# Rotating images by 90 degrees: two of the twelve slabs loaded in rows of 8 KB instead of 16 KB

## The chip, the cores and the metric

The kernel runs on one core of one Trainium2 chip. The metric is the device time in microseconds (us) of one execution. Ratios are computed as the mean time of one kernel's fast runs over that of the kernel before in the same rounds on the same chip, so they are not quite the ratio of the medians that are quoted beside them.

## The reference

The input is `x`, float32 of 32 x 3 x 256 x 256, 25.17 MB. The output has the same size, each image turned by 90 degrees:

```python
def reference(x):
    return np.rot90(x, k=-1, axes=(-2, -1)).astype(np.float32)
```

There is no arithmetic: 25.17 MB come in, 25.17 MB go out, and VectorE rearranges them in between.

## The kernel before

The 96 images are taken in 12 slabs of 8 images (2 MiB). A slab is loaded with two transfers of 1 MiB, in one of two forms. In the *plain* form a transfer fills all 128 partitions with 8 image rows (8 KB, one packet) each. In the *wide* form it fills every second partition with 16 rows (16 KB, one packet), and the second transfer fills the others. Two transposes a slab turn it; their access patterns depend on the form, and their result is the same, so that the stores are the same: 8 KB from each partition.

```python
    RI, RO = 16, 8
    ld8_v = rows_in.rearrange("(n i p r) w -> n p i (r w)", i=I, p=P, r=RO)
    ld16_v = rows_in.rearrange("(n i m r) w -> n i m (r w)", i=I, m=Q * K, r=RI)
    # ... one buffer per slab; 12 x 16 KB in each partition
    for n in range(n_slabs):
        for i in range(I):
            if n in (0, last):
                nc.sync.dma_start(out=units[n][:, i], in_=ld8_v[n][:, i])
            else:
                nc.sync.dma_start(out=units[n][i::I].rearrange("p i f -> p (i f)"), in_=ld16_v[n, i])

    for n in range(n_slabs):
        t_in, t_out = units[n], units[n - 1] if n else turned0
        if n in (0, last):
            # ... two transposes of the plain form
        else:
            # ... two transposes of the wide form
        # ... stores of slab n: slab 1 as 128 KB, 896 KB and 1 MiB, slabs 2 and 3 as 2 x 1 MiB, the rest 2 MiB
    # ... slab 0, turned in PSUM, is copied back by ScalarE and stored last
```

## Time and profile before

| what | value |
|---|---|
| time before, three runs | 123.51, 123.54, 123.78 us |
| span of the profiled execution | 122.3 us |

The prediction below shows the page and the stretches. The waits of the DMA queue (columns: who waited, for what, us in total, times, longest):

```profile
SPq L65 <- DMA u<-in_x_dram: 25.5, 13, 2.0
...
SPq L87 <- DMA u<-in_x_dram: 8.3, 4, 2.1
```

An issue waits for the landing of an earlier transfer. In the trace eight completion semaphores (counters that tell that a transfer has landed) go round among the transfers, so that transfer number j is issued when number j - 8 has landed. That gives a clock: the issue times of the stores are the landing times of the loads eight places ahead. The second view is the timeline of the kernel before around the turn from loads to stores (columns: start, duration, engine, line, operation):

```profile
44.87 0.35 SPq L82 DMA_DIRECT2D out_dram<-u  x1
47.39 0.34 SPq L83 DMA_DIRECT2D out_dram<-u  x1
49.81 0.33 SPq L84 DMA_DIRECT2D out_dram<-u  x1
52.32 7.65 SPq L87 DMA_DIRECT2D out_dram<-u  x4
59.69 1.28 ACT L92 ACT_TABLE_LOAD   x1 [59.69 <-DMA u<-in_x_dram]
62.67 3.31 SPq L89 DMA_DIRECT2D out_dram<-u  x3
```

ScalarE is released at 59.69 us by the first half of the last slab, and the issue at 62.67 us waits for its second half. So the last load of 1 MiB took 62.67 - 59.69 = 2.98 us. Between the issues before it lie 2.42 to 2.52 us.

### The profile page before, as it was taken

Reading aid. Unit: us, or ns where it says so; the run is one execution under the profiler, and the core shown is the slowest. Engines: PE = TensorE matmul, PEld = TensorE weight load, DVE = VectorE, ACT = ScalarE, POOL = GpSimd, SP = SyncE. Lnnn points to the kernel's source line nnn. Section 1 sums busy time; section 2 is a strip of 40 time slices with the busy share of each in tenths; the row PEclk is TensorE's granted clock in tenths of the full one; section 3 lists DMA queues with packets and bytes.
Section 4 is the critical chain, followed back from the end, with each engine's and each line's share of the span. In section 5 each row is a group of like instructions: output and inputs, shape, how many; then the busy total and the mean of one; then the engine's idle time right before and its main releaser. Section 6 shows DMA issues by size and latency. Waiting matters only on the chain.

```text
span 122.3 us, 138 instructions
## 1 busy us (share of the span) xinstructions
DVE 93.3 (76%) x24; ACT 5.0 (4%) x3; POOL 0.2 (0%) x4
## 2 busy tenths in 40 slices
DVE  0199999999999999999999999999999940000000
ACT  0000000000000000000400000000000641000000
POOL 0000000000000000000000000000000000000000
DMA  3999999999999999999999999999999999999994
GB/s 118 418 450 429 429 429 429 429 429 429 429 429 429 429 429 429 429 429 391 359 413 429 429 429 426 429 421 429 429 429 429 429 429 429 429 429 426 429 429 180
DMA packets 5632, 50.33 MB, mean 412 GB/s; under 512 B 640, under 2 KB 768, under 8 KB 896
## 3 DMA queue, kind: packets, MB, share of 16 engines
q1 hardware_dynamic: 5632, 50.33, 97.8%
HBM read 25.17 MB, written 25.17 MB: 412 GB/s over the span
## 4 chain that ended last, share of the span: by engine, by line
DVE 47%; issue 27%; DMA 4%; DVEq 3%; ACT 2%
DVE u L79 37%; DVE turned L73 6%; DMA u<-in_x_dram 4%; DVE u L73 3%; DVEq L119 3%; ACT u L92 2%
## 5 line engine op out<-in xcount | busy, mean ns | idle before, releaser
L79 DVE STREAM_TRANSPOSE u<-u 128x2048 f32<-128x2048 f32 x20 | 78.0, 3949 | 0.3
L73 DVE STREAM_TRANSPOSE turned<-u 128x2048 f32<-128x2048 f32 x2 | 7.6, 3828 | 5.6 <-DMA u<-in_x_dram 5.6
L73 DVE STREAM_TRANSPOSE u<-u 128x2048 f32<-128x2048 f32 x2 | 7.7, 3953 | 0.0
L92 ACT COPY u<-turned 128x2048 f32<-128x2048 f32 x2 | 3.7, 1866 | 36.5 <-DVE u L73 36.5
L92 ACT ACT_TABLE_LOAD x1 | 1.3, 1283 | 59.7 <-DMA u<-in_x_dram 59.7
L108 POOL MEMSET const-bfloat16-1.0<- 128x1 bf16 x1 | 0.1, 102 | 0.0
L108 POOL MEMSET const-uint8-127<- 128x1 uint8 x1 | 0.1, 102 | 0.0
L108 POOL MEMSET const-float32-0.0<- 128x1 f32 x1 | 0.1, 99 | 0.2 <-issue 0.2
L108 POOL MEMSET const-float32-1.0<- 128x1 f32 x1 | 0.1, 99 | 0.0
## 6 DMA issues: line engine op xcount, KB each, us to landing
u<-in_x_dram SPq DMA_DIRECT2D x24, 1024.0 KB, 19.6
out_dram<-u SPq DMA_DIRECT2D x9, 2048.0 KB, 23.0
out_dram<-u SPq DMA_DIRECT2D x5, 1024.0 KB, 17.7
out_dram<-u SPq DMA_DIRECT2D x1, 896.0 KB, 17.8
out_dram<-u SPq DMA_DIRECT2D x1, 128.0 KB, 18.3
```

The lines of the kernel that those rows point to most:

```text
L73: nc.vector.transpose(out=dst[:, :, ::-1, ::-1], in_=src)
L79: nc.vector.transpose(out=dst[:, cs], in_=src[:, cs])
L92: nc.scalar.copy(out=units[last][:, i], in_=turned0[:, i])
L108: nc = _bacc.Bacc("TRN2", target_bir_lowering=False, num_devices=1)
L119: with _tile.TileContext(nc) as tc:
```

## The change

The intent: the plain form was used for the first and the last slab, and it is now used for the last three (6 MiB) and the first, so that slabs 9 and 10 (4 MiB) change. Loads and transposes change their form together; bytes, number of transfers and order stay.

```diff
+    plain = (0, last - 2, last - 1, last)
...
-            if n in (0, last):
+            if n in plain:
                 nc.sync.dma_start(out=units[n][:, i], in_=ld8_v[n][:, i])
...
-        if n in (0, last):
+        if n in plain:
             for i in range(I):
```

## The prediction

> **What bounds the kernel now.** I read the page of the kernel before from the top: busy shares, slices, the DMA queue, then the chain, the groups and the waits of the DMA queue. Busy shares and DMA first:
>
> ```profile
> span 122.3 us, 138 instructions
> ...
> DVE 93.3 (76%) x24; ACT 5.0 (4%) x3; POOL 0.2 (0%) x4
> ...
> DVE  0199999999999999999999999999999940000000
> ...
> DMA  3999999999999999999999999999999999999994
> GB/s 118 418 450 429 429 429 429 429 429 429 429 429 429 429 429 429 429 429 391 359 413 429 429 429 426 429 421 429 429 429 429 429 429 429 429 429 426 429 429 180
> DMA packets 5632, 50.33 MB, mean 412 GB/s; under 512 B 640, under 2 KB 768, under 8 KB 896
> ...
> q1 hardware_dynamic: 5632, 50.33, 97.8%
> ```
>
> VectorE is busy for 76% and is done 20 us before the end: the last tenths of its row are 0. The DMA row is 9 in every slice but the first and the last, and the queue's packets fill 97.8% of 16 engines' span. So the bytes set the time: 25.17 MB in, 25.17 MB out, at 429 GB/s: 50.33 / 0.429 = 117.3 us. The span is 122.3 us; the missing 5.0 us are the ramp at the start, the tail at the end, and one dip in slices 19 to 21 (391, 359, 413 instead of 429). A slice is 122.3 / 40 = 3.06 us, so the dip lies at 55 to 64 us and costs (38 + 70 + 16) / 429 x 3.06 = 0.9 us.
>
> The chain of waits names VectorE for 47%. That is no bound here: the chain can't see the DMA backlog. It goes from the last transpose to the last store's issue at 101.3 us, and nothing in it explains the 21 us until the end. The issues of the DMA queue explain them (median time from issue to landing, last column):
>
> ```profile
> u<-in_x_dram SPq DMA_DIRECT2D x24, 1024.0 KB, 19.6
> out_dram<-u SPq DMA_DIRECT2D x9, 2048.0 KB, 23.0
> out_dram<-u SPq DMA_DIRECT2D x5, 1024.0 KB, 17.7
> ```
>
> 1 MiB at 429 GB/s takes 2.44 us, but a load lands 19.6 us after its issue: about eight transfers are ahead of it at any time. The DMA engines are never out of work, so the moment at which a transpose ends or a store is issued does not matter as long as that backlog (some 18 us of it) is not used up.
>
> The third view is the busy time by stretch (columns: stretch, its length, then busy of VectorE, ScalarE and GpSimd, granted clock, DMA share, GB/s):
>
> ```profile
> 20.00:40.00 20.00, 19.90 (x6) 0.00 (x0) 0.00 (x0) 1.00 1.00 428
> 40.00:56.00 16.00, 15.93 (x5) 0.00 (x0) 0.00 (x0) 1.00 1.00 425
> 56.00:59.00 3.00, 3.00 (x2) 0.00 (x0) 0.00 (x0) 1.00 0.93 391
> 59.00:62.00 3.00, 2.97 (x2) 1.28 (x1) 0.00 (x0) 1.00 1.02 344
> 62.00:80.00 18.00, 17.93 (x6) 0.00 (x0) 0.00 (x0) 1.00 1.01 428
> ```
>
> From 20 to 40 us only the 16 KB packets of the wide loads move: 428 GB/s. From 62 to 80 us only the 8 KB packets of the stores: also 428. Between lie the last two loads (already 8 KB rows) and the first stores; the whole loss is there. The trace's packet records say the same one level down: a 16 KB packet takes 611 ns (median of 1280), an 8 KB one 309 ns (median of 3456, loads and stores), and in the last load, at about 59.3 to 61.3 us, packets of 8 KB took 400 to 700 ns on all engines, some 0.52 us per engine in excess. The packet before it, in the first half of the same slab, is clean at 309.
>
> **What the Trainium skill says.** "DMA: Bandwidth & Descriptors", section "Where 436 GB/s comes from", puts the ceiling at 435 GB/s (16 ports, 32 bytes, 850 MHz) and expects near that rate for large transfers; the 429 here agree, so the steady stages have about 1% left in them, whatever the row length. The same page, "Why small descriptors are slow (HBM only)", gives a fixed overhead of some 3 cycles per packet; in the packet records the spacing of starts is about 306 ns for 8 KB and 608 to 612 ns for 16 KB, so a halved packet costs some 2 to 4 ns extra, which agrees. The same page, "Why a DMA increments its semaphore by 16 and not by 1", says that both 64 and 128 rows are spread over 16 engines; the equal rates of the two forms agree. "SBUF — State Buffer", section "Door 1: The DMA port swizzle", warns that partitions 0 to 63 reach only half the ports. The wide loads have 64 rows too, but on every second partition, over all 128; at 428 GB/s the trace shows no such halving, so there is none that the change could remove.
>
> **The change part by part.**
>
> Loads: slabs 9 and 10 (two transfers of 1 MiB each) go from 64 rows of 16 KB on alternate partitions to 128 rows of 8 KB on all partitions. Removed: 4 x 64 = 256 packets of 16 KB. Added: 4 x 128 = 512 of 8 KB. By durations: 512 x 309 - 256 x 611 = 158.2 - 156.4 = 1.8 us of engine time, over 16 engines 0.11 us, all on the path, as the DMA is. By starts (306 against 610 per 16 KB) it is 256 x 2 / 16 = 0.03 us. I take 0.1 us. Bytes, number of transfers and order of issue stay as they are; the instruction order of the changed program, compared with the old one, shows the same 40 DMA issues, 24 transposes and 2 copies.
>
> Transposes: four of the wide form become four of the plain form, 128x2048 both. The groups give both forms:
>
> ```profile
> L79 DVE STREAM_TRANSPOSE u<-u 128x2048 f32<-128x2048 f32 x20 | 78.0, 3949 | 0.3
> L73 DVE STREAM_TRANSPOSE turned<-u 128x2048 f32<-128x2048 f32 x2 | 7.6, 3828 | 5.6 <-DMA u<-in_x_dram 5.6
> L73 DVE STREAM_TRANSPOSE u<-u 128x2048 f32<-128x2048 f32 x2 | 7.7, 3953 | 0.0
> ```
>
> The row with the same kind of source and destination (units to units) is 3953 against 3949 ns: 4 x 4 ns = 0.02 us, and off the path. A wide slab needs both of its loads before the first transpose, a plain one only one per transpose. That would gain 2.4 us where VectorE waits for loads; here slab 9 lands at about 50 us and is transposed at about 76 us, so there is nothing to gain.
>
> Stores: untouched in shape. They read what the transposes leave, in the same layout.
>
> The turn from loads to stores: the last two loads and the first store, around which the 0.5 us of slow packets and most of the 0.9 us dip lie, are the same before and after. What changes is what runs 2.4 to 12 us ahead of them. With about 16 packets per engine of 8 KB already between the last wide load and the first store, I expect no effect.
>
> Sum: +0.1 (packets) + 0.0 (transposes) + 0.0 (turn) = +0.1 us: 123.54 + 0.1 = 123.64, say 123.6.
>
> **The rivals.** (1) The dip is caused by the switch from 16 KB to 8 KB rows shortly before the stores, or by engines drifting apart in long packets, and the longer run of 8 KB loads smooths it. For it: the dip begins close to the last slab, and whoever tuned this kernel had already made just that slab plain. Against: the first MiB of the last slab runs at 309 ns a packet, and the slow packets come after it, next to the stores. The most it could win is the dip, 0.9 us: 122.7. That is 0.7%, within 2%.
> (2) 8 KB loads are slower in bulk than 16 KB ones. The only 8 KB loads here are 2 MiB at the start (with the ramp) and 2 MiB at the end (with the dip), and both are by an imperfect stage: slices 2 and 3 show 418 and 450. If the reads suffered, say, as in the last MiB (0.5 us each), four of them would cost 2 us: 125.6. Against: the packets of the first MiB of the last slab, and those of the first slab after its ramp, are at 309.
> (3) VectorE becomes the bound, or the stores starve. For that its 93.3 us would have to grow by the 18 us backlog; 0.02 us does not.
> (4) The extra packets shorten how far the queue runs ahead. The waits of the queue show one issue per landed transfer, eight in flight, a count of transfers and not of packets. Nothing changes.
>
> **Range and chances.** The three timed runs span 123.51 to 123.78, the profiled one 124.06, so noise alone is 0.2 to 0.3 us. Down to 123.2 covers a part of rival 1, up to 124.1 a part of rival 2 and noise. Faster by over 2% (below 121.07) would need 2.5 us; the whole distance between the span and the bytes at 429 GB/s is 5.0 us, most of it ramp and tail that the change doesn't touch, and the dip is 0.9: chance 0.01. Slower by over 2% (above 126.0) needs rival 2 at its worst: 0.02. The rest, 0.97, is within 2%.
>
> **What would show it right or wrong.** Right: 5632 + 256 = 5888 packets, 50.33 MB; VectorE 93.3 us; 428 GB/s in 45 to 55 us, now of 8 KB packets; the same dip of about 0.9 us at the turn, at the same place; last store issued at about 101 us, with some 20 us to go. Rival 1 would show as slices of 429 where now 391 and 359 stand; rival 2 as slices 15 to 19 below 425. It would be wrong if 8 KB loads and the write side interact in a way that the steady stages of this trace can't show, since here the two forms never run side by side for long.

## The result, and the profile after

The changed kernel takes 123.72 us in the median of six runs (123.60 to 123.98), the kernel before in the same and the earlier rounds 123.85 us (123.51 to 124.09). The ratio is 0.9996, with a 95% interval of 0.9975 to 1.0017: the same.

The page of the changed kernel, the lines that answer to those of before:

```profile
span 121.8 us, 140 instructions
...
DVE 92.7 (76%) x24; ACT 5.0 (4%) x3; POOL 0.2 (0%) x4
...
GB/s 86 425 436 430 430 430 430 430 430 430 430 430 430 430 430 403 430 422 420 420 397 429 430 425 425 430 425 430 428 430 430 428 430 430 425 425 428 425 430 218
DMA packets 5888, 50.33 MB, mean 413 GB/s; under 512 B 640, under 2 KB 768, under 8 KB 896
...
q1 hardware_dynamic: 5888, 50.33, 98.1%
...
L80 DVE STREAM_TRANSPOSE u<-u 128x2048 f32<-128x2048 f32 x16 | 62.4, 3945 | 0.3
L74 DVE STREAM_TRANSPOSE u<-u 128x2048 f32<-128x2048 f32 x6 | 22.8, 3931 | 0.0
```

There are 256 packets more, as worked out. VectorE is about as busy as before. The total hardly moves, but the GB/s row has another shape: the hole at the turn is shallower (420, 420, 397 where 391, 359, 413 stood), and slices 16 to 18 (403, 430, 422), which stood at 429, are lower. The busy time by stretch of the changed kernel, in the same stretches as in the prediction:

```profile
20.00:40.00 20.00, 19.90 (x6) 0.00 (x0) 0.00 (x0) 1.00 1.01 432
40.00:56.00 16.00, 15.93 (x5) 0.00 (x0) 0.00 (x0) 1.00 1.00 418
56.00:59.00 3.00, 3.00 (x2) 0.00 (x0) 0.00 (x0) 1.00 0.99 412
59.00:62.00 3.00, 2.97 (x2) 1.28 (x1) 0.00 (x0) 1.00 1.01 394
62.00:80.00 18.00, 17.93 (x6) 0.00 (x0) 0.00 (x0) 1.00 1.02 430
```

The last column says that 40 to 56 us, where the new 8 KB loads begin, lost (425 to 418), and that 56 to 62 us won (391 and 344 to 412 and 394). A packet counts where it starts, so a few GB/s in a short stretch mean little; the timeline is sharper:

```profile
49.72 0.33 SPq L85 DMA_DIRECT2D out_dram<-u  x1
52.25 7.74 SPq L88 DMA_DIRECT2D out_dram<-u  x4
59.72 1.28 ACT L93 ACT_TABLE_LOAD   x1 [59.72 <-DMA u<-in_x_dram]
62.34 3.47 SPq L90 DMA_DIRECT2D out_dram<-u  x3
```

The last load now takes 62.34 - 59.72 = 2.62 us instead of 2.98. The four loads ahead of it take longer: from the issue at 49.72 to the landing at 59.72 are 10.00 us, before they were 9.88 (49.81 to 59.69). So two effects of opposite sign may lie under one unchanged time.

### The profile page after: what moved, and what is told of

Read it like the earlier page. It is cut to its first block, busy times and chain, and to the rows that moved or that the text cites. A ratio compares the mean times of both kernels' runs of the same rounds, so it can differ in the third digit from the quotient of the medians.

```text
span 121.8 us, 140 instructions
## 1 busy us (share of the span) xinstructions
DVE 92.7 (76%) x24; ACT 5.0 (4%) x3; POOL 0.2 (0%) x4
## 4 chain that ended last, share of the span: by engine, by line
DVE 41%; issue 33%; DMA 4%; DVEq 3%; ACT 2%
DVE u L80 31%; DVE turned L74 6%; DMA u<-in_x_dram 4%; DVE u L74 4%; DVEq L120 3%; ACT u L93 2%
```

## The experiments

Twelve runs were made, two of them repeats of known kernels, in three batches, each batch on one chip beside the kernel before; all gave the right result. Two theories stood at the start. **A**: loads in 8 KB packets are a little slower, the turn from loads to stores is a little cheaper, and the two cancel. **B**: both differences are accidents of one execution.

### Batch 1: noise, and the two ends of the scale

**The kernel before, again** (no edit).

> The kernel before under another name: the noise floor, and a second profile of the turn from loads to stores. Theory A (the two profiles differ by a small loss in 8 KB loads and by a smaller dip at the turn, and the two cancel) expects ratio 1.000 and the same dip: 391, 359, 413 GB/s in slices 19 to 21, about 0.5 us of excess per engine at the turn. Theory B (both differences are accidents of one execution) expects ratio 1.000 and a dip that looks different from the first profile, by 0.2 us or more.

Ratio 1.0004 (0.9992 to 1.0016), median 123.96 us. The noise floor of a ratio is thus about 0.1%. The dip was there again but shallower: 419, 392, 408 GB/s in slices 19 to 21, with 0.23 us of excess per engine in the packet records (the time of 8 KB packets over 309 ns each), counted over the 4 us around the turn, where the first profile had 0.60 by the same count. This much speaks for B, and it says that one profile of the turn is good to some 0.2 us only.

**The changed kernel, again** (no edit).

> The changed kernel again, timed with five rounds. Theory A: ratio 0.998 to 1.001, with 403 to 422 GB/s again in the slices where the last 6 MiB load, about 0.03 us of excess per engine in every 2 us of them, and a dip at the turn of about 0.2 us. Theory B: ratio 1.000, and a profile in which the 8 KB loads run at 429 or the dip is as in the kernel before.

Ratio 0.9987 (0.9975 to 0.9999), median 123.74 us. Slices 16 to 18 show 411, 422, 425 GB/s: the lower rate of the 8 KB loads is there again, and so is the smaller loss at the turn. This agrees with A.

**Only the first slab plain.**

```diff
-    plain = (0, last - 2, last - 1, last)
+    plain = (0,)
```

> Only the first slab with 8 KB rows; the last one wide like its neighbours, so that 16 KB packets run right up to the stores. Theory A (a run of 8 KB loads ahead of the stores shrinks the dip): the dip grows, from 0.5 to 0.8 us of excess or more; time +0.2 to +0.5 us, ratio 1.002 to 1.004. Theory B (row length does not matter): ratio 1.000, the dip as before.

Ratio 1.0008 (0.9997 to 1.0020), median 123.99 us, not clear of 1 and below the 1.002 to 1.004 of theory A. The GB/s row shows where the loss at the turn goes without plain slabs:

```profile
GB/s 83 426 439 429 434 429 429 429 434 429 434 423 434 429 429 429 429 429 429 364 402 428 429 429 426 426 429 429 429 426 429 429 429 429 426 429 429 429 429 166
```

429 right up to the turn, then 364 and 402. The expected growth of the excess did not come (0.51 us per engine, within the two values of the kernel before); what grew is the spread of the 16 engines, see the table below.

**All slabs plain.**

```diff
-    plain = (0, last - 2, last - 1, last)
+    plain = tuple(range(n_slabs))
```

> All slabs with 8 KB rows, 20 MiB more of them than before. Theory A: an 8 KB load stage loses about 1.5% (0.03 us in 2 us), over 20 MiB at 2.44 us per MiB = 48.9 us that is 0.7 us, plus 1280 more packets at 7 ns over 16 engines = 0.56 us at most, less 0.35 us at the turn: +0.4 to +0.9 us, ratio 1.003 to 1.007, load stages at 420 to 424 GB/s. Theory B: +0.0 to +0.3 us, load stages at 428 or 429.

Ratio 1.0024 (1.0011 to 1.0037), median 124.18 us: slower by a quarter of a per cent, clear of the noise, and less than the 1.003 to 1.007 of theory A. Its GB/s row and its turn:

```profile
GB/s 72 420 428 428 428 428 420 425 425 428 420 412 423 420 425 428 425 417 412 425 421 427 428 428 428 428 428 428 428 428 428 428 428 428 428 428 428 428 428 201
```

```profile
60.55 1.28 ACT L93 ACT_TABLE_LOAD   x1 [60.55 <-DMA u<-in_x_dram]
63.00 3.19 SPq L90 DMA_DIRECT2D out_dram<-u  x3
```

The load half of the row averages some 423 instead of 429. There is no dip at the turn any more: the last load takes 63.00 - 60.55 = 2.45 us. In the trace's records of landings, 1 MiB landed every 2.485 us in the 8 KB loads and every 2.446 us in the 16 KB loads of the other kernels (each the mean over the 16 engines). That is A, and it has its first price: 0.039 us per MiB loaded in 8 KB packets, or 1.6%. The stores, 8 KB packets as well, run at 4.90 us per 2 MiB, thus 2.45 per MiB: they don't pay it.

### Batch 2: packet or partition, near or far, and VectorE

**8 KB packets in the wide layout.** The plain form differs from the wide one in packet size and in the partitions that it writes. Here the kernel before has its wide loads cut into 8 KB packets, the second half of each row first, with the same partitions and the same result:

```diff
-                nc.sync.dma_start(out=units[n][i::I].rearrange("p i f -> p (i f)"), in_=ld16_v[n, i])
+                nc.sync.dma_start(
+                    out=units[n][i::I][:, ::-1],
+                    in_=ld16_v[n, i].rearrange("m (h f) -> m h f", h=I)[:, ::-1],
+                )
```

> The kernel before with every wide load cut into 8 KB packets, second half of each 16 KB row first, so that partitions, bytes and result stay and only the packet size changes (20 MiB of it). Theory S (the 1.6% that 8 KB loads lose belongs to the packet size): 1 MiB lands every 2.485 us instead of 2.447, load stage +0.76 us, and the last load ahead of the stores 2.5 us as in the kernel with all slabs plain: ratio about 1.002 to 1.004. Theory P (it belongs to writing all 128 partitions instead of every second one): 1 MiB still every 2.447 us, the last load as in the kernel before (2.8 to 3.0 us): ratio 1.000.

Ratio 1.0028 (1.0015 to 1.0041), median 124.12 us; 6912 packets, as with all slabs plain; 1 MiB every 2.485 us; the last load 2.49 us. Both the price and the cheap turn come with the packet size (theory S). Which partitions are written makes no difference here. (The reversed order of the halves is a second difference of this kernel, but the kernel with all slabs plain, which hasn't it, shows the same 2.485 us.)

**All plain except the last slab**, which is wide, so that 16 KB packets stand next to the stores (edit: `plain = tuple(range(last))`).

> All slabs plain except the last one, which is wide. Theory N (the dip at the turn comes from the packets right next to the stores): a last load of 2.8 us or more and engines that spread to about 1 us at the turn, as with only the first slab plain; time +0.7 (20 MiB less 2 of 8 KB loads at 0.038 us) over the kernel before or more, ratio 1.004 to 1.007. Theory R (it shrinks with the length of the run of 8 KB loads, wherever it ends): a last load of 2.5 to 2.6 us, ratio 1.001 to 1.003.

Ratio 1.0024 (1.0010 to 1.0038), median 124.09 us. The last load took 2.44 us, the steady rate of wide loads, with no loss at all, and less than the 2.5 to 2.6 us of theory R. So the loss at the turn is not made by the packets next to the stores (theory N falls). It depends on what ran earlier.

**More work for VectorE** in the changed kernel: the transposes of slab 4, or of slabs 4, 5 and 6, are done twice, with the same result.

```diff
-            for h in range(2):
+            for h in (0, 1, 0, 1) if n in (4,) else (0, 1):
```

> The changed kernel with the two transposes of slab 4 done twice: VectorE +7.9 us, all later stores issued 7.9 us later. If the backlog of the DMA queue hides VectorE: same time, ratio 0.998 to 1.001, last store issued at about 108.4 us instead of 100.5. If the chain of waits is right that VectorE is on the path: +7.9 us, ratio 1.06.

> The same with the transposes of slabs 4, 5 and 6 done twice: VectorE +23.6 us. The last store would be issued at about 124 us; two stores of 2 MiB (4.9 us each) follow the last transpose, so by the backlog account the span is about 124 + 5 to 10 us, 129 to 134 us: ratio 1.06 to 1.10, of 23.6 us only some 8 to 12 us show. VectorE on the path throughout: +23.6 us, ratio 1.19.

With two transposes more: ratio 0.9982 (0.9963 to 1.0002), median 123.57 us, no loss against the kernel before of the same batch (123.78; the changed kernel itself did not run in it). VectorE was busy for 100.4 us instead of 92.7, 7.7 us more. Its last store was issued at 108.26 us:

```profile
108.26 0.37 SPq L94 DMA_DIRECT2D out_dram<-u  x1
```

With six more: ratio 1.0958 (1.0940 to 1.0976), median 135.64 us, and this is what a used-up backlog looks like:

```profile
DVE 115.8 (87%) x30; ACT 5.0 (4%) x3; POOL 0.2 (0%) x4
...
DMA  3999999999999999999999999997929295684995
GB/s 122 429 468 392 470 392 470 392 465 397 451 411 441 407 429 416 414 426 411 426 431 431 421 421 426 426 424 311 392 103 406 118 392 235 274 353 179 409 431 235
```

The last third of the GB/s row has holes, where the engines wait for the next store. Of 115.8 - 92.7 = 23.1 us more of VectorE, 123.78 x 0.0958 = 11.9 us show in the time; some 11 us are hidden. VectorE is off the path in the changed kernel, with about that much to spare, though the chain of waits gives it 41% of the span there. The chain of the kernel before gives it 47%; no work was added to that kernel, and that VectorE is off its path too is argued from the same DMA row and the same time.

### Batch 3: what the loss at the turn depends on

Theory **D** said that the loss builds up with the 16 KB packets since the last 8 KB stage, theory **T** that the total of 8 KB packets before the turn decides, wherever they lie.

**Slabs 0 to 8 plain, the last three wide** (`plain = tuple(range(last - 2))`).

> Slabs 0 to 8 plain, the last three wide (6 MiB of 16 KB packets ahead of the stores). The last of them took 2.44 us where only 2 MiB were wide, 2.82 where 22 MiB were. Theory D (the loss at the turn builds up with the MiB of 16 KB packets since the last 8 KB stage): last load 2.5 to 2.7 us. Theory T (the total of 8 KB packets, 18 MiB here, decides wherever they lie): 2.44 to 2.47. Loads by 8 KB packets: 14 MiB more than before at 0.038 us, +0.53 us, less 0.3 to 0.5 at the turn: ratio 1.000 to 1.003.

**Slabs 0 to 5 plain, the last six wide** (`plain = tuple(range(last - 5))`), and its mirror, **slab 0 and the last six plain** (`plain = (0, *range(last - 5, n_slabs))`).

> Slabs 0 to 5 plain, the last six wide (12 MiB of each). Theory D: last load 2.7 us or more, engines spread as in the kernel before, +0.3 us, ratio 1.002 to 1.004. Theory T: as plain_last6, which has nearly the same totals.

> The mirror of wide_last6: slab 0 and the last six plain, 12 MiB of 8 KB ahead of the stores. Both theories: last load 2.5 to 2.55 us, between the changed kernel (2.60) and all plain (2.49); 10 MiB more of 8 KB at 0.038 us = +0.38 us less 0.4 at the turn: ratio 0.999 to 1.002. Slower than the changed kernel by 0.1 to 0.3 us.

**Slabs 9 and 10 plain, the last one wide** (`plain = (0, last - 2, last - 1)`), a candidate for a better version.

> Slabs 9 and 10 plain, the last one wide: a candidate for a better version, as the wide last load after a plain run took 2.44 us. 2 MiB more of 8 KB than before, +0.08 us; if the plain run of 4 MiB is enough for a last load of 2.6 us or less, -0.3 us: ratio 0.997 to 0.999. If the packets next to the stores matter after such a short run, 2.8 us and ratio 1.000 to 1.001.

The ratios are 1.0021 (1.0007 to 1.0035), 1.0000 (0.9987 to 1.0014), 1.0003 (0.9991 to 1.0016) and 0.9988 (0.9976 to 1.0001), in this order. The table has all kernels of this series, worked out from the traces' records of landings, each landing being the mean over the 16 engines. "Loss in loads" is the time from the landing of load 0 to that of load 22, less 22 x 2.446 us. "Last load" is from load 22 to load 23. "Sum" is the loss in loads plus what the last load took over 2.446. "Spread" is the time between the first and the last engine to land the last transfer of all. Two or three values are two or three profiles.

| plain slabs | MiB in 8 KB | loss in loads, us | last load, us | sum, us | spread, us | ratio |
|---|---|---|---|---|---|---|
| 0 | 2 | 0.08 | 2.82 | 0.45 | 1.03 | 1.0008 |
| 0, 11 (before) | 4 | 0.16, 0.12 | 3.00, 2.77 | 0.71, 0.44 | 0.90, 0.76 | 1.0004 |
| 0, 9, 10 | 6 | 0.22 | 2.59 | 0.37 | 0.50 | 0.9988 |
| 0, 9 to 11 (after) | 8 | 0.26, 0.25, 0.25 | 2.60, 2.59, 2.59 | 0.42, 0.39, 0.40 | 0.49, 0.60, 0.41 | 0.9996, 0.9987 |
| 0 to 5 | 12 | 0.45 | 2.45 | 0.45 | 0.32 | 1.0000 |
| 0, 6 to 11 | 14 | 0.48 | 2.51 | 0.55 | 0.38 | 1.0003 |
| 0 to 8 | 18 | 0.66 | 2.45 | 0.66 | 0.47 | 1.0021 |
| 0 to 10 | 22 | 0.82 | 2.44 | 0.82 | 0.29 | 1.0024 |
| all | 24 | 0.86 | 2.49 | 0.90 | 0.55 | 1.0024 |
| 0, 11, others 8 KB in the wide layout | 24 | 0.85 | 2.49 | 0.90 | 0.33 | 1.0028 |

(The third value of the changed kernel is from the run with two transposes more. The run with six more, whose stores starve at the end, is left out; its loads give 0.26, 2.57 and 0.38 us.) Theory D falls: with 12 MiB of 16 KB packets ahead of the stores, the last load still takes 2.45 us, as long as 12 MiB of 8 KB packets came first. T fits all rows. The loss in loads grows evenly with the MiB in 8 KB packets, and the loss at the turn shrinks with them, until it is gone at 12 MiB or so; 8 KB packets beyond that only cost. Up to 14 MiB the sum stays at 0.37 to 0.55 us, the first profile of before apart. It looks like a debt of about 0.45 us that is paid either at the turn or bit by bit. The same rows allow a second reading, which no run here separates from it: up to 14 MiB the last load lands 56.6 to 56.8 us after load 0 (57.0 in the first profile of before), so it may be held back until about that time by something else, and wait less when the loads before it come late. To delay the loads by other means than the packet size would test it. The engines' spread is a second, small part: it grows at the turn where the loss there is large, stays until the end (0.76 to 1.03 us against 0.29 to 0.60), and the last engine ends the run.

What the debt is, in the hardware, these runs don't show. That the 16 engines had drifted apart before the turn doesn't explain it: at load 22 their spread was 0.47 us with only the first slab plain, where the last load took 2.82 us, and 0.48 us with all slabs plain, where it took 2.49. No run isolated it, and the sum rests on one profile for most rows.

The candidate with slabs 9 and 10 plain has the lowest sum and 123.53 us against 123.68 of the kernel before, but its interval reaches 1 and overlaps that of the changed kernel. No version here beats both kernels clearly.

## Why the prediction was right or wrong

The time was right: 123.72 us against 123.6 foretold, within 2%. Two of its steps were not as it put them, and their errors have opposite signs. That the sum came out so near is thus luck in part.

**The bound**: "So the bytes set the time" fits the two runs with more VectorE work: 7.7 us more of it cost nothing, so VectorE doesn't set it. The spare time was put too high: "some 18 us of it". The queue is 18 us deep per transfer, but stores are issued every 7.8 us in the end and drained in 4.9, so the depth shrinks towards the end, and of a delay of 23.1 us some 11 us were hidden.

**Loads**: the step had "I take 0.1 us" for the extra packets. The size was near: the loss in loads of the table grew by 0.09 to 0.15 us, and 4 MiB x 0.039 us would be 0.16. The reasons failed. "428 GB/s in 45 to 55 us, now of 8 KB packets" came out as about 422 (1 MiB in 2.485 us), so the steady stages did not run alike "whatever the row length".

The prediction took its figures for an 8 KB packet mostly from stores: the 306 ns are the pace of the stores (4.90 us per 2 MiB, 16 packets an engine), of the 3456 packets with the median of 309 ns only 512 are loads, and the stretch from 62 to 80 us has stores alone (with slab 1's packets of 1 and 7 KB among them). From these figures it read "some 2 to 4 ns extra, which agrees"; 2 x 306 less 608 to 612 is 0 to 4, and for loads the landings give 2 x 2.485 / 8 less 2.446 / 4, some 10 ns. The price could be seen in the kernel before: load 22, of 8 KB packets and ahead of the turn, landed 2.48 us after load 21 in its first profile and 2.49 in its second, although the packets looked "clean at 309" in the first.

Rival 2 was right in kind and far too large in size: 0.04 us per MiB, not 0.5.

**The turn**: this is the step that failed. "With about 16 packets per engine of 8 KB already between the last wide load and the first store, I expect no effect." The last load went from 2.77 to 3.00 us down to 2.59 to 2.60, so 0.2 to 0.4 us came back. The step supposed that only what lies next to the stores can matter; the run with all but the last slab plain and the one with the last six wide show that it doesn't have to lie there. Rival 1 named the smoothing by a longer run of 8 KB loads, but the causes that it gave don't fit: a switch of rows near the stores doesn't go with the loss (16 KB rows stood right before the stores both with only the first slab plain, 2.82 us, and with the last six wide, 2.45 us), nor does a spread of the engines ahead of the turn. Why the turn gets cheaper stays open.

**Transposes**: +0.02 us was foretold; the page shows 92.7 us busy instead of 93.3, and the last store issued at 100.5 us instead of 101.3. The step compared how long one transpose takes (3953 and 3949 ns), but their records overlap a little: in the changed kernel six plain ones in a row take 22.77 us, 3.80 each, and 16 wide ones 62.60, 3.91 each. It is off the path, as the step said.

**The sum** was +0.1 us; the pieces measured give +0.1 to +0.16 for the loads and -0.2 to -0.4 for the turn, thus about 0 to -0.3 us, and the two ratios, 0.9996 and 0.9987, give -0.05 and -0.16 us. A change of this size is at the edge of what five rounds show.

## What to carry to other kernels

When a change leaves the time alone, the slices can still show two effects that cancel; a scale from none to all of it, with a few points between, separated them here better than repetition did. An engine that the chain of waits names for half the span may have 11 us to spare: add work to it and see. And a rate measured on stores was no evidence here for loads of the same packet size; the time between landings showed what the packet durations hid.

## What the Trainium skill lacked or had wrong

- "DMA: Bandwidth & Descriptors", section "Why small descriptors are slow (HBM only)": it gives a fixed overhead of about 3 cycles per packet and doesn't tell loads from stores. Going from 16 KB to 8 KB packets adds 4 packets per engine and MiB, and at the 850 MHz of its section "Where 436 GB/s comes from" (if that is the clock of these cycles) that is an estimated 4 x 3.5 = 14 ns; the loads here lost 39 ns per MiB (2.485 against 2.446 us), so this overhead alone doesn't account for them. Stores in 8 KB packets (2.45 us per MiB) showed no such loss, though none in 16 KB packets was run beside them.
- The same page, and any other that I read, has nothing on the turn from loads to stores in a full queue: it cost 0.3 to 0.55 us here (a last load of 2.77 to 3.00 us instead of 2.45), with a spread of the 16 engines of 0.76 to 1.03 us at the end, and with 12 MiB or more of the loads in 8 KB packets the last load took 2.44 to 2.51 us.
- "SBUF — State Buffer", section "Summary: rules for kernel authors": it advises 32 partitions over 64, at the same rate. What it measured are neighbouring partitions; the rule doesn't say that 64 alternate partitions over the whole range can be as good as 128, and no run here tried 64 neighbouring ones: 1 MiB landed every 2.446 us in the wide loads, 429 GB/s, the rate of the stores from all 128.
